# Hybrid decoder trunk on one core: queries left unnormalised until the softmax, and one 512-column product in the channel sub-layers

## The chip, the cores and the metric

One core of one Trainium2 chip runs the whole program in a single launch. The metric is the device time in microseconds (us), the median of several executions; the profile is of one more execution.

## The reference

Two layers work on a sequence of 256 tokens of width 1024, all in float32. Each layer is a mixing sub-layer and a channel sub-layer:

```
h = adaLN(rms_norm(x)); proj = h @ w_in        # q,k,v of A, q,k,v of B, two gates
q_a = rope(rms_norm(q_a), positions)           # rms_norm over each head's 64 numbers
k_a = rope(rms_norm(k_a), positions)           # the same for q_b, k_b
y_a = softmax([mask(q_a k_a^T / 8), sink]) v_a # 8 query heads, 2 key heads, window 128
y_b = softmax(mask(q_b k_b^T / 8)) v_b         # 8 heads, causal (one block of 256)
x  += gt1 * ((sig(gate_a)*(y_a @ w_oA) + sig(gate_b)*(y_b @ w_oB)) @ w_out)
h   = adaLN(rms_norm(x)); x += gt2 * (relu(h @ w_up)**2 @ w_down)   # w_up 1024x4096
```

The scale and the shift of adaLN and the gains gt1, gt2 are products of silu(c) with w_ada (1024x6144 per layer).

## The kernel before, in words

**Precision.** Every large product runs as three products of float32r parts: an operand is split into a high part (a rounded copy) and a low part (the rest). The activations h live transposed in `hT_hi` and `hT_lo`, [128, 8, 256] each; a weight piece of 1024 columns is cast by ScalarE (L440, high part) and subtracted by VectorE (L446, low part) into a slot of 2x1024 numbers. With the activations as moving operand, `mm3f` (L526 to L529) makes high x high, high x low and low x high, each a matmul of 256 columns with its own weight load, all into the same 256 columns of a PSUM tile.

**Feature products.** `feat_half` (L617) makes one block of 128 output features for all 256 tokens: 8 blocks k of the contraction, 3 matmuls each. The gates of the mixing sub-layer are 16 such blocks per layer (L1105); in the channel sub-layer `up` (L1173) makes 2 blocks per step f, for f = 2 to 15, so 28 per layer and 56 in all. `up_done` (L1162) then runs in three stages: Relu from PSUM on ScalarE; Square and a cast to `uhi` on ScalarE; the subtraction to `ulo` on VectorE. `out_product` (L643) makes step f+2 before it multiplies step f by w_down, in 48 matmuls of 512 columns (`out_half`, L522 to L524).

**Queries and keys.** `head_norm_rope` (L735) takes two PSUM tiles (128 tokens each) of a projection: squares on ScalarE (L744), sums by head and an added eps on VectorE (L748, L750), the power -0.5 on GpSimd (L751), the product with it (L758, `qn`), the rotary products (L766 `ra`, L771 `rb`) and their sum (L785 `ro`) on VectorE, and transposes on TensorE (L793). Kinds 0 and 2 are the queries of A and B, 1 and 3 the keys; the gains sit in the rotary tables. `attn_pair` (L799) takes two heads: scores (L810), mask and row maximum (L815, L817), the negated and scaled maximum (L823 or L827), Exp with a constant scale and the maximum as its per-row bias (L830, L832), the row sums, transposes (L854) and the product with v (L870).

**What sets the order.** The bodies are generators on a list `bg`; each `tick()` (L171) inside the large products advances every generator by one stage, splits a weight piece on every second tick, and advances one `ada_unit` (L242) of the list `slow`: VectorE multiplies a w_ada piece of 128x512 by a column of silu(c) and adds it up (L259), 8 steps a unit. A scheduler then orders each engine's queue, so an edit moves rows on every engine. At a boundary between sub-layers `residual` (L637), `ln_stats` (L534) and `ln_apply` (L562) make the next hT from the last products, and `proj_first` (L712) begins the next product with what is ready. All weights come through the one queue of SyncE (`load_next`, L409; `ada_load`, L210).

Of the kernel before, what the change touches and what calls it, by code (L numbers as in the profile page):

```python
# [8 lines left out]
F32 = mybir.dt.float32  # L9
F32R = mybir.dt.float32r  # L10
# [5 lines left out]
P = 128  # L16
S = 256
# [61 lines left out]
def kernel(ctx: ExitStack, tc: tile.TileContext, io):  # L79
# [537 lines left out]
    def feat_half(ahi, alo, ps, k0=0):  # L617

        slot, hi, lo = stream.get()
        for k in range(KT):  # L620
            mm3f(ps, hi[:, k, :], lo[:, k, :], ahi[:, k, :], alo[:, k, :], k == 0, k == KT - 1)
            if k == KT - 1:
                stream.release(slot)
            if k % 4 == 3:
                tick()

    def out_half(accs, half, uhi, ulo, left, k, first, last, ts_, hs_, ticks=True):
        slot, hi, lo = half
# [103 lines left out]
        return ps  # L732


    def head_norm_rope(pss, nh, tabs, kind, dst, p0, dup):  # L735
# [4 lines left out]
        rs = small.tile([P, NT, nh], F32, tag=f"rs{nh}", name=nm("rs"), bufs=2)  # L740
        sqs = []
        for t in range(NT):
            sq = ring(w, "sq")
            nc.scalar.activation(sq, pss[t], AF.Square)  # L744
            sqs.append(sq)
        yield
        for t in range(NT):
            nc.vector.tensor_reduce(out=ss[:, t, :], in_=sqs[t].rearrange("p (h d) -> p h d", d=HD),  # L748
                                    axis=AX.X, op=ALU.add)
        nc.vector.tensor_scalar(out=ss, in0=ss, scalar1=HD * EPS, scalar2=None, op0=ALU.add)  # L750
        nc.gpsimd.tensor_tensor(out=rs, in0=ss, in1=mhalf[:, :NT * nh].rearrange("p (t h) -> p t h", h=nh), op=ALU.pow)  # L751
        for _ in range(POW_LAG):
            yield
        q3s, ab = [], []
        for t in range(NT):
            q3 = ring(w, "qn").rearrange("p (h d) -> p h d", d=HD)
            with tc.issue_after(stream.last):
                nc.vector.tensor_tensor(out=q3, in0=pss[t].rearrange("p (h d) -> p h d", d=HD),  # L758
                                        in1=rs[:, t, :][:, :, None].to_broadcast([P, nh, HD]), op=ALU.mult)
            q3s.append(q3)  # L760
# [36 lines left out]


    def attn_pair(l, pair, qT, kT, v_sb, ahi, alo, alloc):  # L799
# [12 lines left out]
        for i in range(2):  # L812
# [5 lines left out]
                                           in1=(mask[:, 0:2 * P] if swa else mask[:, 2 * P:4 * P]), scale=1.0,  # L818
                                           scalar=NEG, op0=ALU.add, op1=ALU.max, accum_out=mx[:, i, 1:2])
            sms.append(sm)  # L820
        if swa:
            ns = nsink[:, l, 2 * pair:2 * pair + 2][:, :, None].to_broadcast([P, 2, NT])
            nc.vector.scalar_tensor_tensor(out=nmx, in0=mx, scalar=-SCALE, in1=ns, op0=ALU.mult, op1=ALU.min)  # L823
            es = small.tile([P, 2, NT], F32, tag="es", name=nm("es"))
            nc.vector.tensor_tensor(out=es, in0=nmx, in1=ns, op=ALU.subtract)
        else:
            nc.vector.tensor_scalar(out=nmx, in0=mx, scalar1=-SCALE, scalar2=None, op0=ALU.mult)  # L827
        yield
        for i in range(2):
            nc.scalar.activation(sms[i][:, 0:P], sms[i][:, 0:P], AF.Exp, bias=nmx[:, i, 0:1], scale=SCALE,  # L830
                                 accum_out=rsum[:, i, 0:1])
            nc.scalar.activation(sms[i][:, P:3 * P], sms[i][:, P:3 * P], AF.Exp, bias=nmx[:, i, 1:2], scale=SCALE,  # L832
                                 accum_out=rsum[:, i, 1:2])
        if swa:
            nc.scalar.activation(es, es, AF.Exp)
# [205 lines left out]
    def mixing(l, rest, finish):  # L1041
# [118 lines left out]

    def mlp(l, rest, finish, new_u):
        def up_done(uhi, ulo, left, jj, ps):  # L1162
            r = ring(S, "relu")
            nc.scalar.activation(r, ps, AF.Relu)  # L1164
            yield
            u = ring(S, "usq")
            nc.scalar.activation(u, r, AF.Square)
            nc.scalar.copy(uhi[:, jj, :], u)
            yield
            nc.vector.tensor_tensor(out=ulo[:, jj, :], in0=u, in1=uhi[:, jj, :].bitcast(F32), op=ALU.subtract)  # L1170
            left[0] -= 1

        def up(f):  # L1173
            u = new_u()
            for jj in range(2):
                ps = tmp_t()[:, :S]
                feat_half(hT_hi, hT_lo, ps)
                bg.insert(0, up_done(*u, jj, ps))
            return u

# [92 lines left out]
```

## Time and profile before

| | us |
|---|---|
| median of 3 runs | 757.29 |
| the three runs | 754.62, 758.05, 757.29 |
| the profiled execution | 755.65 |
| its span, first to last instruction | 753.9 |

A stretch of the span is named by its start and end, as 226 to 353, in us. In it: the start and the projections of layer 0 (0 to 60), the rest of that mixing sub-layer (60 to 206), its channel sub-layer (206 to 397), the mixing sub-layer of layer 1 (397 to 564) and its channel sub-layer (564 to 754). A matmul's listed duration covers its pipeline, so two neighbours overlap; the step from one start to the next is what it takes of the engine. Rows of waits give the engine that stood idle and what ended it.

### The profile page before, as it was taken

Reading aid. Unit: us, or ns where it says so; the run is one execution under the profiler, and the core shown is the slowest. Engines: PE = TensorE matmul, PEld = TensorE weight load, DVE = VectorE, ACT = ScalarE, POOL = GpSimd, SP = SyncE. Lnnn points to the kernel's source line nnn. Section 1 sums busy time; section 2 is a strip of 40 time slices with the busy share of each in tenths; the row PEclk is TensorE's granted clock in tenths of the full one; section 3 lists DMA queues with packets and bytes.
Section 4 is the critical chain, followed back from the end, with each engine's and each line's share of the span. In section 5 each row is a group of like instructions: output and inputs, shape, how many; then the busy total and the mean of one; then the engine's idle time right before and its main releaser. Section 6 shows DMA issues by size and latency. Waiting matters only on the chain.

```text
span 753.9 us, 12320 instructions
## 1 busy us (share of the span) xinstructions
PE 730.7 (97%) x4713; PEld 645.3 (86%) x4713; DVE 587.2 (78%) x1090; ACT 431.2 (57%) x817; POOL 32.0 (4%) x24
## 2 busy tenths in 40 slices
PE   7999889999999999999999999999999999999997
PEld 6678778899778999989977888989988899999896
DVE  6598998999899988988789788987879745545542
ACT  6545579863466655455436357576447755555550
POOL 1003200000000000000000401000000000000000
PEclk9999999999999999999999999999999999999999
DMA  8996758877949999989882633844662865565501
GB/s 293 392 325 227 227 162 285 274 254 248 303 128 330 370 347 299 332 309 342 283 318 98 224 119 113 263 157 166 225 223 80 269 203 175 182 207 172 189 33 57
DMA packets 110538, 173.46 MB, mean 230 GB/s; under 512 B 4744, under 2 KB 68488, under 8 KB 110480
## 3 DMA queue, kind: packets, MB, share of 16 engines
q1 hardware_dynamic: 109744, 172.54, 67.9%
q8 instruction: 37, 0.61, 0.3%
q10 hardware_dynamic: 736, 0.15, 0.1%
q14 instruction: 21, 0.17, 0.1%
HBM read 171.62 MB, written 1.05 MB: 229 GB/s over the span
## 4 chain that ended last, share of the span: by engine, by line
PE 72%; DVE 13%; DMA 7%; ACT 3%; issue 2%; POOL 2%; SPq 0%; ACTq 0%; DVEq 0%; POOLq 0%
PE tmp L527 11%; PE acc L524 11%; PE acc L522 11%; PE acc L523 11%; PE tmp L528 10%; PE tmp L529 10%; DMA araw<-in_w_ada_dram 4%; DVE ada L259 2%; DVE w L446 2%; PE acc L984 2%; POOL rs L751 1%; ACT w L440 1%; PE tmp L870 1%; DMA wraw<-in_w_up_dram 1%; PE acc L810 1%
## 5 line engine op out<-in xcount | busy, mean ns | idle before, releaser
L446 DVE TENSOR_TENSOR w<-wraw,w 128x1024 fp32r<-128x1024 f32 x137 | 166.3, 1221 | 48.1 <-ACT w L440 46.8
L440 ACT CAST w<-wraw 128x1024 fp32r<-128x1024 f32 x150 | 155.9, 1048 | 78.9 <-PE acc L524 44.5
L527 PE MATMUL tmp<-hT_hi,w 128*128 128x256 f32 x480 | 140.1, 292 | 1.3 <-DVE alo L874 1.2
L529 PE MATMUL tmp<-hT_hi,w 128*128 128x256 f32 x480 | 135.9, 283 | 0.0
L528 PE MATMUL tmp<-hT_lo,w 128*128 128x256 f32 x480 | 135.7, 283 | 0.0
L259 DVE SCALAR_TENSOR_TENSOR ada<-araw,cs,ada 128x512 f32<-128x512 f32 x140 | 104.4, 746 | 3.2 <-DMA araw<-in_w_ada_dram 2.1
L527 PEld LDWEIGHTS tmp<-hT_hi,w 128*128 128x128 f32 x480 | 91.5, 191 | 8.2 <-issue 4.4
L528 PEld LDWEIGHTS tmp<-hT_lo,w 128*128 128x128 f32 x480 | 91.7, 191 | 0.7
L529 PEld LDWEIGHTS tmp<-hT_hi,w 128*128 128x128 f32 x480 | 91.6, 191 | 0.3 <-issue 0.3
L522 PE MATMUL acc<-w,uhi 128*128 128x512 f32 x192 | 75.4, 393 | 0.0
L523 PE MATMUL acc<-w,uhi 128*128 128x512 f32 x192 | 74.9, 390 | 0.0
L524 PE MATMUL acc<-w,ulo 128*128 128x512 f32 x192 | 74.9, 390 | 0.0
L1164 ACT ACTIVATE relu<-tmp 128x256 f32<-128x256 f32 x56 | 21.5, 384 | 68.8 <-PE tmp L529 68.8
L524 PEld LDWEIGHTS acc<-w,ulo 128*128 128x128 f32 x192 | 36.1, 188 | 7.6
L522 PEld LDWEIGHTS acc<-w,uhi 128*128 128x128 f32 x192 | 36.1, 188 | 6.9
L523 PEld LDWEIGHTS acc<-w,uhi 128*128 128x128 f32 x192 | 36.1, 188 | 6.8
L440 ACT CAST kv<-wraw 128x1024 fp32r<-128x1024 f32 x21 | 22.1, 1051 | 24.6 <-PE acc L524 19.8
L446 DVE TENSOR_TENSOR ahi<-wraw,ahi 128x1024 fp32r<-128x1024 f32 x18 | 22.0, 1222 | 15.0 <-ACT ahi L440 14.9
L446 DVE TENSOR_TENSOR kv<-wraw,kv 128x1024 fp32r<-128x1024 f32 x21 | 25.7, 1222 | 9.9 <-ACT kv L440 9.8
L446 DVE TENSOR_TENSOR qT<-wraw,qT 128x1024 fp32r<-128x1024 f32 x21 | 25.6, 1220 | 8.3 <-ACT qT L440 8.3
L527 PE MATMUL tmp<-hT_hi,alo 128*128 128x256 f32 x112 | 31.8, 284 | 0.0
L528 PE MATMUL tmp<-hT_lo,alo 128*128 128x256 f32 x112 | 31.7, 283 | 0.0
(248 smaller groups left out, 1744.8 us busy)
## 6 DMA issues: line engine op xcount, KB each, us to landing
araw<-in_w_ada_dram SPq DMA_DIRECT2D x80, 512.0 KB, 5.9
wraw<-in_w_up_dram SPq DMA_DIRECT2D x32, 1024.0 KB, 5.9
wraw<-in_w_down_dram SPq DMA_DIRECT2D x32, 1024.0 KB, 5.9
wraw<-in_w_in_dram SPq DMA_DIRECT2D x28, 1024.0 KB, 5.7
wraw<-in_w_out_dram SPq DMA_DIRECT2D x8, 1024.0 KB, 5.6
wraw<-in_w_in_dram SPq DMA_DIRECT2D x12, 512.0 KB, 7.1
wraw<-in_w_o_swa_dram SPq DMA_DIRECT2D x8, 512.0 KB, 3.3
wraw<-in_w_o_moba_dram SPq DMA_DIRECT2D x8, 512.0 KB, 5.1
```

Of the source, the lines that this page charges most:

```text
L259: nc.vector.scalar_tensor_tensor(out=acc, in0=raw[:, k, :], scalar=cs[:, kk:kk + 1], in1=(bz if kk == 0 else acc), op0=ALU.mult, op1=ALU.add)
L440: nc.scalar.copy(hi, r)
L446: ins = nc.vector.tensor_tensor(out=lo, in0=r, in1=hi.bitcast(F32), op=ALU.subtract)
L522: nc.tensor.matmul(ps, lhsT=lh, rhs=rh, start=start, stop=False)
L523: nc.tensor.matmul(ps, lhsT=lh, rhs=rl, start=False, stop=False)
L524: nc.tensor.matmul(ps, lhsT=ll, rhs=rh, start=False, stop=stop)
L527: nc.tensor.matmul(ps, lhsT=wh, rhs=ah, start=start, stop=False)
L528: nc.tensor.matmul(ps, lhsT=wh, rhs=al, start=False, stop=False)
L529: nc.tensor.matmul(ps, lhsT=wl, rhs=ah, start=False, stop=stop)
L751: nc.gpsimd.tensor_tensor(out=rs, in0=ss, in1=mhalf[:, :NT * nh].rearrange("p (t h) -> p t h", h=nh), op=ALU.pow)
L984: T.matmul(ps[t], lhsT=left[:, 2 * q + k, t * P:(t + 1) * P], rhs=w[:, k, :], start=(first and k == 0), stop=(last and k == 1))
L1164: nc.scalar.activation(r, ps, AF.Relu)
```

## The change

The activations' parts become one tile, so that both parts of one k lie side by side as 512 columns. `feat_wide` makes high weights times both in one matmul, and low weights times the high part in a second one; `wide_sum` copies the upper half out of PSUM on ScalarE and adds the lower half on VectorE, in two stages. Only `up` uses it: `WIDE_GATE` is False for both layers, so the gates stay as they were. For the queries the product `qn` is left out; the rotary products read PSUM, and the power (now of the sums times 64) goes into the maximum and into Exp as a per-row scale.

```diff
+WIDE_GATE = (False, False)
...
-    hT_hi = state.tile([P, KT, S], F32R, name="hT_hi")
-    hT_lo = state.tile([P, KT, S], F32R, name="hT_lo")
+    hT = state.tile([P, KT, 2, S], F32R, name="hT")
+    hT_hi, hT_lo = hT[:, :, 0, :], hT[:, :, 1, :]
...
+    def feat_wide(ps):
+        slot, hi, lo = stream.get()
+        for k in range(KT):
+            nc.tensor.matmul(ps, lhsT=hi[:, k, :], rhs=hT[:, k].rearrange("p a s -> p (a s)"), start=k == 0, stop=False)
+            nc.tensor.matmul(ps[:, :S], lhsT=lo[:, k, :], rhs=hT_hi[:, k, :], start=False, stop=k == KT - 1)
...
+    def wide_sum(ps, r):
+        nc.scalar.copy(r, ps[:, S:])
+        yield
+        nc.vector.tensor_tensor(out=r, in0=ps[:, :S], in1=r, op=ALU.add)
+        yield
...
+        query = kind % 2 == 0
...
+            if query:
+                nc.vector.tensor_scalar(out=ss, in0=ss, scalar1=HD * EPS, scalar2=1.0 / SCALE ** 2, op0=ALU.add,
+                                        op1=ALU.mult)
+                rq[kind] = rs
...
+        squares()
         q3s, ab = [], []
+        if query:
+            q3s = [p.rearrange("p (h d) -> p h d", d=HD) for p in pss]
+        else:
+            yield
+            powers()
...
         yield
         for t in range(NT):
...
+        if query:
+            powers()
...
+        rp = rq[0 if swa else 2][:, :, h0:h0 + 2].rearrange("p t i -> p i t")
         if swa:
-            nc.vector.scalar_tensor_tensor(out=nmx, in0=mx, scalar=-SCALE, in1=ns, op0=ALU.mult, op1=ALU.min)
+            nc.vector.scalar_tensor_tensor(out=nmx, in0=mx, scalar=-1.0, in1=rp, op0=ALU.mult, op1=ALU.mult)
+            nc.vector.tensor_tensor(out=nmx, in0=nmx, in1=ns, op=ALU.min)
...
-            nc.scalar.activation(sms[i][:, 0:P], sms[i][:, 0:P], AF.Exp, bias=nmx[:, i, 0:1], scale=SCALE,
+            nc.scalar.activation(sms[i][:, 0:P], sms[i][:, 0:P], AF.Exp, bias=nmx[:, i, 0:1], scale=rp[:, i, 0:1],
...
         def up_done(uhi, ulo, left, jj, ps):
-            r = ring(S, "relu")
-            nc.scalar.activation(r, ps, AF.Relu)
-            yield
+            r = ring(S, "usum")
+            yield from wide_sum(ps, r)
+            nc.scalar.activation(r, r, AF.Relu)
...
-                ps = tmp_t()[:, :S]
-                feat_half(hT_hi, hT_lo, ps)
+                ps = tmp_t()
+                feat_wide(ps)
```

**Place 1.** VectorE's queue before, layer 0, from the sums of the squares of `qb` (`ss_623`) and `kb` (`ss_629`) to the rotary products; `acc_282`, `acc_283` hold qb, `acc_284`, `acc_285` kb, `w` is a weight piece's low part.

```order
L748 TENSOR_REDUCE ss_629<-sq_631 128x8
L750 TENSOR_SCALAR ss_623<-ss_623 128x16
L446 TENSOR_TENSOR w_4_647<-wraw_510,w_4_647 128x1024
L748 TENSOR_REDUCE ss_629<-sq_633 128x8
L259 SCALAR_TENSOR_TENSOR ada_721<-araw_722,cs,bz 128x512
L750 TENSOR_SCALAR ss_629<-ss_629 128x16
L446 TENSOR_TENSOR w_4_682<-wraw_510,w_4_682 128x1024
L758 TENSOR_TENSOR qn_687<-acc_282,rs_624 128x512
L758 TENSOR_TENSOR qn_689<-acc_283,rs_624 128x512
L758 TENSOR_TENSOR qn_691<-acc_284,rs_630 128x512
L758 TENSOR_TENSOR qn_693<-acc_285,rs_630 128x512
L766 TENSOR_TENSOR ra_705<-qn_687,ct_463 128x512
```

The same place after the change (qb is `acc_281`, `acc_282`; kb `acc_283`, `acc_284`; the sums of kb are `ss_628`, those of qb `ss_622`):

```order
L805 TENSOR_TENSOR ra_649<-acc_281,ct_462 128x512
L810 TENSOR_TENSOR rb_650<-acc_281,st_463 128x8x32 x2
L447 TENSOR_TENSOR w_4_646<-wraw_509,w_4_646 128x1024
L774 TENSOR_REDUCE ss_628<-sq_630 128x8
L774 TENSOR_REDUCE ss_628<-sq_632 128x8
L805 TENSOR_TENSOR ra_670<-acc_282,ct_462 128x512
L781 TENSOR_SCALAR ss_628<-ss_628 128x16
L810 TENSOR_TENSOR rb_671<-acc_282,st_463 128x8x32 x2
L447 TENSOR_TENSOR w_4_687<-wraw_509,w_4_687 128x1024
L774 TENSOR_REDUCE ss_622<-sq_624 128x8
L774 TENSOR_REDUCE ss_622<-sq_626 128x8
L826 TENSOR_TENSOR ro_696<-ra_649,rb_650 128x512
```

The rotary products of qb stand ahead of the sums, kb's sums ahead of qb's, and the first `ro` of qb ahead of every `qn`.

**Place 2.** ScalarE's queue in the channel sub-layer of layer 0, after the change, for the two blocks of one step (`L641` copies the upper half, `L441` casts a weight piece):

```order
L641 COPY usum_3875<-tmp_3841 128x256
L441 CAST w_19_4028<-wraw_3892 128x1024
L1217 ACTIVATE usum_3875<-usum_3875 128x256
L641 COPY usum_3905<-tmp_3866 128x256
L1219 ACTIVATE usq_3908<-usum_3875 128x256
L441 CAST w_19_4052<-wraw_3892 128x1024
L1220 CAST uhi_3839<-usq_3908 128x256
```

Before, the Relu read PSUM and waited for TensorE alone; now the Relu (L1217) waits for VectorE's sum, and the second block's copy and the next weight cast stand behind it.

**Place 3.** VectorE's queue after the change at the end of that sub-layer, from the normalisation of the first 128 tokens (L553) to that of the second:

```order
L553 TENSOR_SCALAR ln_4097<-x_sb,lnr_4122 128x512 x2
L260 SCALAR_TENSOR_TENSOR ada_4941<-araw_4693,cs,ada_4941 128x512
L581 TENSOR_SCALAR ln_4097<-tmp_4147,s_1_0_99,sh_0_103 128x128 x2
L588 CAST hT<-ln_4097 128x2x128
L659 TENSOR_TENSOR res_4164<-acc_2495,gt_2602 128x512
...
L553 TENSOR_SCALAR ln_4097<-x_sb,lnr_4194 128x512 x2
L260 SCALAR_TENSOR_TENSOR ada_4941<-araw_4693,cs,ada_4941 128x512
L260 SCALAR_TENSOR_TENSOR ada_4941<-araw_4942,cs,ada_4941 128x512
```

Before, no `ada` step stood between these rows: all had been queued ahead of the first L552.

## Rows read from the trace of the kernel before

**Rows 1.** The page's head and part 1: busy time, share of span, instructions.

```profile
span 753.9 us, 12320 instructions
PE 730.7 (97%) x4713; PEld 645.3 (86%) x4713; DVE 587.2 (78%) x1090; ACT 431.2 (57%) x817; POOL 32.0 (4%) x24
```

**Rows 2.** Busy time by stretch: start:end, length, each engine, TensorE's granted clock, DMA share, GB/s.

```profile
60.00:108.00 48.00, 41.75 (x281) 35.55 (x279) 43.28 (x96) 26.16 (x56) 12.48 (x4) 1.00 0.59 191
108.00:165.00 57.00, 55.80 (x465) 50.01 (x461) 51.03 (x135) 48.18 (x132) 0.00 (x0) 1.00 0.81 263
226.00:353.00 127.00, 127.00 (x821) 115.98 (x820) 113.25 (x160) 71.90 (x118) 0.00 (x0) 1.00 0.96 333
353.00:404.00 51.00, 48.37 (x278) 41.84 (x277) 42.73 (x69) 23.72 (x44) 1.47 (x2) 1.00 0.78 271
584.00:735.00 151.00, 151.00 (x969) 137.94 (x968) 78.56 (x91) 86.39 (x142) 0.00 (x0) 1.00 0.55 179
```

**Rows 3.** TensorE in order of time: nine starts at 512 columns, then 47 at 256.

```profile
289.93 0.39 PE L522 MATMUL acc<-kv,uhi 128*128 128x512 f32 x1
...
291.75 0.39 PE L524 MATMUL acc<-kv,ulo 128*128 128x512 f32 x1
...
292.09 0.28 PE L528 MATMUL tmp<-hT_lo,w 128*128 128x256 f32 x1
...
297.61 0.28 PE L529 MATMUL tmp<-hT_hi,w 128*128 128x256 f32 x1
```

**Rows 4.** TensorE's waits, 60 to 108: us in total, times, longest.

```profile
PE tmp L854 <- ACT sm L845: 1.8, 1, 1.8
PE tmp L793 <- DVE ro L785: 1.6, 2, 1.1
PE acc L810 <- DVE qn L758: 1.2, 1, 1.2
PE acc L523 <- DVE w L446: 0.9, 2, 0.6
PE acc L810 <- ACT kv L795: 0.6, 1, 0.6
```

**Rows 5.** VectorE's waits, 60 to 108.

```profile
DVE qn L758 <- POOL rs L751: 4.7, 3, 2.8
```

**Rows 6.** Groups by line and shape: count, busy us, mean ns, idle before.

```profile
L1167 ACT ACTIVATE usq<-relu 128x256 f32<-128x256 f32 x56 | 23.4, 419 | 0.1
L1170 DVE TENSOR_TENSOR ulo<-usq,uhi 128x256 fp32r<-128x256 f32 x56 | 23.4, 418 | 5.1 <-ACT uhi L1168 5.1
L1164 ACT ACTIVATE relu<-tmp 128x256 f32<-128x256 f32 x56 | 21.5, 384 | 68.8 <-PE tmp L529 68.8
L832 ACT ACTIVATE sm<-sm,nmx 128x256 f32<-128x256 f32 x32 | 16.0, 500 | 0.0
L970 ACT ACTIVATE hT_hi<-ln,sh,s 128x256 fp32r<-128x256 f32 x8 | 4.4, 593 | 5.4 <-DVE s L304 5.4
L766 DVE TENSOR_TENSOR ra<-qn,ct 128x512 f32<-128x512 f32 x12 | 8.2, 682 | 0.0
L758 DVE TENSOR_TENSOR qn<-acc,rs 128x512 f32<-128x512 f32 x12 | 7.7, 686 | 11.2 <-POOL rs L751 11.2
L823 DVE SCALAR_TENSOR_TENSOR nmx<-mx,nsink 128x4 f32<-128x4 f32 x8 | 1.3, 158 | 0.1
```

**Rows 7.** VectorE's waits, 226 to 353, the longest, and its group of ulo there.

```profile
DVE w L446 <- ACT w L440: 7.1, 7, 1.9
L1170 DVE TENSOR_TENSOR ulo<-usq,uhi 128x256 fp32r<-128x256 f32 x22 | 9.2, 417 | 0.7 <-ACT uhi L1168 0.7
```

**Rows 8.** The boundary from layer 0 to layer 1, in order of time, with waits.

```profile
397.27 0.66 PE L570 MATMUL tmp<-cpack,ln 128*128 128x128 f32 x4 [2.43 <-DVE ln L552]
404.28 0.73 DVE L580 TENSOR_SCALAR ln<-tmp,s,sh 128x128 f32<-128x128 f32 x2 [0.85 <-PE tmp L570]
```

More of the change, by code (lines that the diff above doesn't have):

```diff
@@ L625, in feat_half @@
                 tick()
+    def feat_wide(ps):
[3 more added lines that the diff above has]
+            nc.tensor.matmul(ps[:, :S], lhsT=lo[:, k, :], rhs=hT_hi[:, k, :], start=False, stop=k == KT - 1)
+            if k == KT - 1:
+                stream.release(slot)
+            if k % 4 == 3:
+                tick()
+    def wide_sum(ps, r):
[3 more added lines that the diff above has]
+        yield
     def out_half(accs, half, uhi, ulo, left, k, first, last, ts_, hs_, ticks=True):
@@ L732, in proj_first @@
         return ps
+    rq = {}
     def head_norm_rope(pss, nh, tabs, kind, dst, p0, dup):
@@ L738, in head_norm_rope @@
         w = nh * HD
+        query = kind % 2 == 0
         ss = small.tile([P, NT, nh], F32, tag=f"ss{nh}", name=nm("ss"), bufs=2)
-        rs = small.tile([P, NT, nh], F32, tag=f"rs{nh}", name=nm("rs"), bufs=2)
+        rs = small.tile([P, NT, nh], F32, tag=("rq" if query else f"rs{nh}"), name=nm("rs"), bufs=2)
         sqs = []
[L742 to L745, printed above, removed]
-        yield
-        for t in range(NT):
-            nc.vector.tensor_reduce(out=ss[:, t, :], in_=sqs[t].rearrange("p (h d) -> p h d", d=HD),
-                                    axis=AX.X, op=ALU.add)
@@ L750, in head_norm_rope, with squares @@
-        nc.vector.tensor_scalar(out=ss, in0=ss, scalar1=HD * EPS, scalar2=None, op0=ALU.add)
-        nc.gpsimd.tensor_tensor(out=rs, in0=ss, in1=mhalf[:, :NT * nh].rearrange("p (t h) -> p t h", h=nh), op=ALU.pow)
-        for _ in range(POW_LAG):
-            yield
[L754 to L760, printed above, removed]
+        def squares():
+            for t in range(NT):
+                sq = ring(w, "sq")
+                nc.scalar.activation(sq, pss[t], AF.Square)
+                sqs.append(sq)
@@ new lines, in powers @@
+        def powers():
+            for t in range(NT):
+                nc.vector.tensor_reduce(out=ss[:, t, :], in_=sqs[t].rearrange("p (h d) -> p h d", d=HD),
+                                        axis=AX.X, op=ALU.add)
+            if query:
[3 more added lines that the diff above has]
+            else:
+                nc.vector.tensor_scalar(out=ss, in0=ss, scalar1=HD * EPS, scalar2=None, op0=ALU.add)
+            nc.gpsimd.tensor_tensor(out=rs, in0=ss, in1=mhalf[:, :NT * nh].rearrange("p (t h) -> p t h", h=nh),
+                                    op=ALU.pow)
@@ new lines, in head_norm_rope @@
+        squares()
+        q3s, ab = [], []
+        if query:
+            q3s = [p.rearrange("p (h d) -> p h d", d=HD) for p in pss]
+        else:
+            yield
+            powers()
+            for _ in range(POW_LAG):
+                yield
+            for t in range(NT):
+                q3 = ring(w, "qn").rearrange("p (h d) -> p h d", d=HD)
+                with tc.issue_after(stream.last):
+                    nc.vector.tensor_tensor(out=q3, in0=pss[t].rearrange("p (h d) -> p h d", d=HD),
+                                            in1=rs[:, t, :][:, :, None].to_broadcast([P, nh, HD]), op=ALU.mult)
+                q3s.append(q3)
@@ L826, in attn_pair @@
         else:
-            nc.vector.tensor_scalar(out=nmx, in0=mx, scalar1=-SCALE, scalar2=None, op0=ALU.mult)
+            nc.vector.scalar_tensor_tensor(out=nmx, in0=mx, scalar=-1.0, in1=rp, op0=ALU.mult, op1=ALU.mult)
         yield
         for i in range(2):
-            nc.scalar.activation(sms[i][:, 0:P], sms[i][:, 0:P], AF.Exp, bias=nmx[:, i, 0:1], scale=SCALE,
+            nc.scalar.activation(sms[i][:, 0:P], sms[i][:, 0:P], AF.Exp, bias=nmx[:, i, 0:1], scale=rp[:, i, 0:1],
                                  accum_out=rsum[:, i, 0:1])
-            nc.scalar.activation(sms[i][:, P:3 * P], sms[i][:, P:3 * P], AF.Exp, bias=nmx[:, i, 1:2], scale=SCALE,
+            nc.scalar.activation(sms[i][:, P:3 * P], sms[i][:, P:3 * P], AF.Exp, bias=nmx[:, i, 1:2], scale=rp[:, i, 1:2],
                                  accum_out=rsum[:, i, 1:2])
@@ L1101, in gate_done @@
         def gate_done(j, ps):
+            if WIDE_GATE[l]:
+                r = ring(S, "gsum")
+                yield from wide_sum(ps, r)
+                ps = r
             nc.scalar.activation(th[:, j, :], ps, AF.Tanh, scale=0.5)
@@ L1105, in mixing @@
         for j in range(16):
-            ps = tmp_t()[:, :S]
-            feat_half(hT_hi, hT_lo, ps)
+            ps = tmp_t()
+            if WIDE_GATE[l]:
+                feat_wide(ps)
+            else:
+                ps = ps[:, :S]
+                feat_half(hT_hi, hT_lo, ps)
             bg.insert(0, gate_done(j, ps))
@@ L1162, in up_done @@
         def up_done(uhi, ulo, left, jj, ps):
-            r = ring(S, "relu")
-            nc.scalar.activation(r, ps, AF.Relu)
-            yield
+            r = ring(S, "usum")
+            yield from wide_sum(ps, r)
+            nc.scalar.activation(r, r, AF.Relu)
             u = ring(S, "usq")
@@ L1175, in up @@
             for jj in range(2):
-                ps = tmp_t()[:, :S]
-                feat_half(hT_hi, hT_lo, ps)
+                ps = tmp_t()
+                feat_wide(ps)
                 bg.insert(0, up_done(*u, jj, ps))
```

1 line of the change is left out of this document (added).

## The prediction, made before the changed kernel had run

> **What bounds the kernel now.** I read the page's head first: TensorE is busy for 730.7 of 753.9 us, VectorE for 587.2, ScalarE for 431.2 [rows 1]. That leaves TensorE at most 23.2 us of visible idleness, so what the kernel does on TensorE sets its time almost everywhere, and a change must either take steps off TensorE or take away one of its few waits. The table by stretches says where these waits lie [rows 2]. From 584 to 735 (the channel sub-layer of layer 1) TensorE never stands still and VectorE is busy for 78.56 of 151 us: whatever leaves TensorE there leaves the time. From 226 to 353 (the same sub-layer of layer 0) TensorE is also full, but VectorE, which does the steps of w_ada there as well, is busy for 113.25 of 127 us and the DMA share is 0.96: there is little room beside TensorE. From 60 to 108 TensorE is busy for 41.75 of 48 us, and this is where the queries and keys of layer 0 are normalised. The granted clock is 1.00 in every stretch, the upper of its two levels, and no row suggests that the change touches it.
>
> Then I looked at what a matmul takes of TensorE. Its listed duration covers its pipeline, so I took the starts [rows 3]: eight steps at 512 columns take 1.82 us, 227.5 ns each; 46 steps at 256 columns take 5.52 us, 120.0 ns each. Two matmuls of 256 columns take 240 ns where one of 512 takes 227.5: 12.5 ns go with the instruction and not with the columns.
>
> **The channel sub-layers: TensorE.** A block had 8 x 3 matmuls of 256 columns; now it has 8 of 512 and 8 of 256. The columns are the same, and 8 instructions are gone, as are their weight loads. There are 56 blocks (28 per layer), so 448 matmuls fewer, each worth 12.5 ns: **5.6 us**, half in each layer. The Trainium skill's "TensorE: Matmul & The Clock Gate", section "Wait — 56ns, not 53.3ns?", speaks against it: a warm matmul costs its columns and a fixed 2.5 ns or so. By that figure the 448 would give an estimated 1.1 us, and the sum below would end at 754.0. This trace disagrees with 12.5 ns, and the sum goes by that.
>
> **The channel sub-layers: what is added.** Per block ScalarE gets one more instruction: the copy from PSUM costs what the Relu from PSUM costs, 384 ns, and the Relu now reads SBUF, as the Square does, at 419 ns [rows 6]. That is 56 x 0.42 = 23.5 us. ScalarE is busy for 71.90 of 127 us from 226 to 353, where 22 blocks would add 9.2 us, and for 86.39 of 151 in layer 1 [rows 2]; TensorE's stream covers it. VectorE gets one addition of 256 columns per block, as the `ulo` subtraction costs: 418 ns [rows 6]. In layer 1 the idle 72 us of VectorE cover it. In layer 0 they are tight: 22 blocks lie between 226 and 353 [rows 7], so 22 x 0.417 = 9.2 us of work go into 127 - 113.25 = 13.75 us of idle time, in a stretch that shrinks by 22 x 8 x 12.5 ns = 2.2 us. That leaves 2.3 us. Most of the idle time is waiting for ScalarE's cast of a weight piece, 7.1 us of it in seven waits of at most 1.9 us [rows 7], and that cast waits for TensorE to free a slot: VectorE is early there, not late, so I take the idle time as usable. But the wait is new (place 2): the Relu stands behind VectorE's sum, and with it the next copy and weight cast; TensorE waits for these last, after it has used up the weight slots already filled.
>
> The scheduler has moved some w_ada steps behind the boundary (place 3). One step of w_ada now stands between the normalised rows and hT for the first 128 tokens, and two for the second. In order they add about 0.67 us (the chain was already late there: TensorE waits 2.43 us for L552 [rows 8]) and 1.3 us less the 0.85 us for which VectorE waited there anyway [rows 8], so 0.5 us. Its saved 2.8 us in layer 0 also reach that boundary as an earlier arrival of TensorE, before a VectorE that has more to do. A bound below is nothing lost; a bound above is that all 2.8 us go and the 1.2 us come on top, 4.0 us. I take **1.5 us lost**, the 1.2 us and a little for the new waits, since the slots hide the rest.
>
> **The queries.** Removed: the product `qn` for the queries, two of 128x512 for each of qa and qb in two layers, 8 x 0.686 = 5.5 us of VectorE [rows 6]. The rotary products then read PSUM; `qn` itself read PSUM and cost 686 ns where `ra` from SBUF cost 682 [rows 6], so they cost the same. Added: one small minimum for each of 8 pairs, 8 x 0.158 = 1.3 us [rows 6]. Moved: the sums and the power, off the chain to the rotary products. In layer 0 VectorE waited 4.7 us for GpSimd's power in three waits [rows 5]; with the four `qn` of that layer, 2.7 us, up to 7.4 us of VectorE's time come back in a stretch where it was busy for 43.28 of 48 us. What TensorE gets of it is bounded by its own waits there [rows 4], 6.1 us in all. The wait for `qn` (1.2) goes, because the rotary products free the projection's PSUM without the power. The waits for `ro` (1.6) go, because qb's `ro` now stands ahead of every `qn` (place 1). Next in line are kb's power, which no longer queues behind qb's on GpSimd, and the weight pieces; of the other 3.3 us I take a third. Bounds: nothing, if kb and the weights take the place of qb at each wait; 6.1 us, if all go. I take **4.0 us**. In layer 1 TensorE is full beside the queries: nothing.
>
> Exp gets a per-row scale beside its per-row bias. The nearest rows are Exp at 256 columns with one per-row operand, 500 ns, and the activation L970 at 256 columns with two, 593 ns [rows 6]: 93 ns for each of 64, 6.0 us of ScalarE. Half fall in layer 0, where ScalarE is busy for 48.18 of 57 us from 108 to 165 [rows 2] but TensorE for 55.80, the gates' products covering it. Bounds: nothing, and the 3.0 us of layer 0 if that cover is gone; I take **0.3 us lost**.
>
> The moved tile adds no copy: hT is written in the same pieces, and I cost it at nothing, since each part still waits for its own writer.
>
> **The sum.** 755.65 - 5.6 + 1.5 - 4.0 + 0.3 = 747.85 us, against the profiled execution (755.65, of which 753.9 is the span). The median of the three runs is 1.64 us above that execution, so I expect a median of **749.5 us**, 1.0% faster. About 0.5%, 3.8 us, is what a measurement of this kernel can tell from no change.
>
> **The rivals.**
>
> *A, the queries give nothing.* VectorE's saved time goes to kb, whose power starts only a little earlier, and to the weight pieces, so TensorE waits as long at other places. For it: two of the five waits are for weight pieces and for kb's transposes copied out (0.9 and 0.6 us [rows 4]). Against it: half of the waits name the queries' own chain. Then 749.5 + 4.0 = 753.5 us, at the edge of no change. Chance 0.19.
>
> *B, the 12.5 ns don't come back.* If the price went with something else than the count of matmuls (the weight's change, which remains twice per k), the 5.6 us shrink to nothing: 755.1 us. Against it: it is the same at 256 and at 512 columns in [rows 3]. Chance 0.05. The Trainium skill's "TensorE: Matmul & The Clock Gate", section named above, would put the kernel near this rival.
>
> *C, VectorE becomes the bound of layer 0's channel sub-layer, and the kernel is slower.* If VectorE's 13.75 us of idle time are forced, because each wait for a cast comes at its place in the queue whatever stands before it, the 9.2 us of sums are added to the stretch, and 6 x 0.42 = 2.5 us to the rest; layer 0 keeps none of its 2.8 us. The sum is 755.65 - 2.8 - 4.0 + 0.3 + 11.7 = 760.85, by the median 762.5 us. It decides from the point where more than 2.3 us of the idle time stay; the whole gain is lost only when some 10 us do. For it: DMA share 0.96 and the new wait of ScalarE on VectorE. Against it: these waits are of an engine that is early. Chance 0.08.
>
> *D, everything goes.* All 6.1 us of the waits, and nothing is lost in layer 0: 755.65 - 5.6 - 6.1 = 743.95, by the median 745.6 us. Chance 0.12.
>
> The forecast has 0.56. The range: from 744.5, a little below D, to 755.5, above A and B; left out are C and what lies between. Faster by over 0.5% (below 753.5): the forecast, D, half of A and a little of the others, 0.78. Slower by over 0.5%: most of C, 0.07. Between: 0.15.
>
> **What would show it.** In the profile after, the starts inside a block should alternate by 227 and 120 ns, and the stretch of layer 1's channel sub-layer should be 2.8 us shorter with TensorE still full. VectorE should show no wait for GpSimd before the rotary products of a query, and TensorE's waits of [rows 4] for `qn` and `ro` should be gone, with under 2.5 us left. Exp should take some 590 ns at 256 columns. In layer 0's channel sub-layer VectorE should be busy for over 95% of the time, and TensorE's wait at the boundary should be 3 to 6 us instead of 2.43. Waits of TensorE for weight pieces inside that sub-layer would mean C; the same total of waits from 60 to 108 would mean A; a step of 240 ns for the wide matmul would mean B.

## The result, and the profile of the changed kernel

The changed kernel takes **752.23 us** (median of 14 runs, 749.42 to 757.62), the kernel before 756.89 (14 runs, 754.62 to 760.76). The ratio is 0.994, with a 95% interval of 0.9916 to 0.9964: 4.7 us, or 0.6%. The forecast was 749.5 with a range of 744.5 to 755.5. The direction and the range hold; of the 7.8 us that the sum had gained, some 3 are missing. The profiled execution took 750.69 us.

The page's head and part 1, which answer to [rows 1]:

```profile
span 748.9 us, 11477 instructions
PE 732.1 (98%) x4265; PEld 625.1 (83%) x4265; DVE 603.6 (81%) x1146; ACT 451.6 (60%) x873; POOL 33.3 (4%) x24
```

TensorE has 448 matmuls fewer (4713 to 4265), and only 16.8 us of visible idleness instead of 23.2. VectorE and ScalarE work 16.4 and 20.4 us more. The stretches, columns as in [rows 2]:

```profile
60.00:108.00 48.00, 46.01 (x320) 40.16 (x319) 48.00 (x111) 31.39 (x69) 10.10 (x4) 1.00 0.70 231
108.00:165.00 57.00, 55.48 (x453) 49.53 (x452) 48.28 (x129) 47.97 (x123) 0.00 (x0) 1.00 0.74 250
226.00:353.00 127.00, 127.00 (x652) 107.76 (x651) 120.14 (x180) 78.78 (x139) 0.00 (x0) 1.00 0.94 327
...
584.00:735.00 151.00, 151.00 (x759) 127.67 (x758) 87.00 (x110) 90.43 (x164) 0.00 (x0) 1.00 0.53 172
```

From 60 to 108 TensorE is busy for 46.01 us where it was 41.75, and all of its waits there are these, against the five of [rows 4]:

```profile
PE acc L851 <- ACT kv L836: 0.8, 1, 0.8
PE acc L851 <- DVE mx L858: 0.8, 1, 0.8
PE tmp L898 <- ACT sm L889: 0.3, 1, 0.3
```

The waits for `qn` and `ro` are gone, 6.1 us have become 1.9, and VectorE waits for GpSimd nowhere in that stretch [rows 5]. In layer 0's channel sub-layer VectorE is busy for 120.14 of 127 us and TensorE never stands still. The added instructions, groups by line as in [rows 6]:

```profile
L1217 ACT ACTIVATE usum<-usum 128x256 f32<-128x256 f32 x56 | 23.3, 417 | 7.5 <-DVE usum L643 7.5
...
L641 ACT COPY usum<-tmp 128x256 f32<-128x256 f32 x56 | 20.8, 372 | 67.0 <-PE tmp L634 67.0
L876 ACT ACTIVATE sm<-sm,nmx,rs 128x256 f32<-128x256 f32 x32 | 18.9, 592 | 0.0
```

```profile
L643 DVE TENSOR_TENSOR usum<-tmp,usum 128x256 f32<-128x256 f32 x56 | 23.6, 422 | 26.5 <-ACT usum L641 26.3
```

Copy 372, sum 422, Relu 417, Exp 592 ns: each within 13 ns of the row it was priced by. The last columns are new waits between the two engines (VectorE 26.3 us for the copy, ScalarE 7.5 for the sum); TensorE, which has its slots filled ahead, waits for neither. At the two boundaries, TensorE in order of time:

```profile
205.42 1.09 PE L571 MATMUL tmp<-cpack,ln 128*128 128x128 f32 x8 [2.37 <-DVE ln L553]
...
392.66 0.63 PE L571 MATMUL tmp<-cpack,ln 128*128 128x128 f32 x4 [0.49 <-DVE ln L553]
```

The second answers to [rows 8]: 0.49 us instead of 2.43, where 3 to 6 had been forecast. The first, within layer 0, I had not looked at; it was 1.70 us in the kernel before (at 207.53), and 2.43 in a second profile of it. And in layer 1, sixteen pairs of a wide and a narrow product (two blocks):

```profile
599.73 0.39 PE L633 MATMUL tmp<-hT,w 128*128 128x512 f32 x1
599.96 0.28 PE L634 MATMUL tmp<-hT,w 128*128 128x256 f32 x1
...
605.37 0.40 PE L523 MATMUL acc<-w,uhi 128*128 128x512 f32 x1
```

(605.37 - 599.73) / 16 = 352.5 ns a pair. By [rows 3] it was to be 227.5 + 120.0 = 347.5, and three narrow products were 360.

### The profile page after: what moved, and what is told of

It reads as the page before. It is cut to its first block, busy times and chain, and to the rows that moved or that the text cites. A ratio compares the mean times of both kernels' runs of the same rounds, so it can differ in the third digit from the quotient of the medians.

```text
span 748.9 us, 11477 instructions
## 1 busy us (share of the span) xinstructions
PE 732.1 (98%) x4265; PEld 625.1 (83%) x4265; DVE 603.6 (81%) x1146; ACT 451.6 (60%) x873; POOL 33.3 (4%) x24
## 4 chain that ended last, share of the span: by engine, by line
PE 83%; DVE 11%; DMA 3%; issue 2%; ACT 1%; POOL 0%; ACTq 0%; DVEq 0%; POOLq 0%; SPq 0%
PE tmp L633 14%; PE acc L523 12%; PE acc L525 12%; PE acc L524 12%; PE tmp L634 7%; PE tmp L528 5%; PE tmp L529 4%; PE tmp L530 4%; PE acc L1028 3%; DVE w L447 2%; DVE ada L260 2%; PE tmp L914 2%; DMA araw<-in_w_ada_dram 1%; PE acc L851 1%; PE tmp L898 1%
## 5 line engine op out<-in xcount | busy, mean ns | idle before, releaser
L441 ACT CAST w<-wraw 128x1024 fp32r<-128x1024 f32 x150 | 155.8, 1048 | 78.4 <-PE acc L525 41.5
L633 PE MATMUL tmp<-hT,w 128*128 128x512 f32 x224 | 80.1, 399 | 0.0
L528 PE MATMUL tmp<-hT,w 128*128 128x256 f32 x256 | 76.7, 299 | 1.5 <-DVE alo L918 1.5
L530 PE MATMUL tmp<-hT,w 128*128 128x256 f32 x256 | 72.4, 283 | 0.1
L529 PE MATMUL tmp<-hT,w 128*128 128x256 f32 x256 | 72.3, 282 | 0.0
L634 PE MATMUL tmp<-hT,w 128*128 128x256 f32 x224 | 62.9, 281 | 0.0
L641 ACT COPY usum<-tmp 128x256 f32<-128x256 f32 x56 | 20.8, 372 | 67.0 <-PE tmp L634 67.0
L528 PEld LDWEIGHTS tmp<-hT,w 128*128 128x128 f32 x256 | 48.6, 190 | 8.3 <-issue 5.3
L633 PEld LDWEIGHTS tmp<-hT,w 128*128 128x128 f32 x224 | 42.1, 188 | 10.0
L530 PEld LDWEIGHTS tmp<-hT,w 128*128 128x128 f32 x256 | 48.7, 190 | 0.7 <-DVE w L447 0.7
L529 PEld LDWEIGHTS tmp<-hT,w 128*128 128x128 f32 x256 | 48.7, 190 | 0.4 <-issue 0.2
L643 DVE TENSOR_TENSOR usum<-tmp,usum 128x256 f32<-128x256 f32 x56 | 23.6, 422 | 26.5 <-ACT usum L641 26.3
L634 PEld LDWEIGHTS tmp<-hT,w 128*128 128x128 f32 x224 | 42.3, 189 | 0.5
L633 PE MATMUL tmp<-hT,alo 128*128 128x512 f32 x112 | 40.3, 399 | 0.0
```

The source lines that it names most:

```text
L441: nc.scalar.copy(hi, r)
L528: nc.tensor.matmul(ps, lhsT=wh, rhs=ah, start=start, stop=False)
L529: nc.tensor.matmul(ps, lhsT=wh, rhs=al, start=False, stop=False)
L530: nc.tensor.matmul(ps, lhsT=wl, rhs=ah, start=False, stop=stop)
L633: nc.tensor.matmul(ps, lhsT=hi[:, k, :], rhs=hT[:, k].rearrange("p a s -> p (a s)"), start=k == 0, stop=False)
L634: nc.tensor.matmul(ps[:, :S], lhsT=lo[:, k, :], rhs=hT_hi[:, k, :], start=False, stop=k == KT - 1)
```

## The experiments

Ratios are to the kernel before on the same chip. The rows come from three chips' runs, four rows each, with 6 or 12 runs a row; the medians of the kernel before there were 758.1, 756.31 and 757.34 us.

| kernel | median us | ratio | 95% interval |
|---|---|---|---|
| the kernel before, again | 758.58 | 1.0001 | 0.9979 to 1.0023 |
| queries' part alone | 754.84 | 0.9972 | 0.9949 to 0.9995 |
| wide products alone | 755.80 | 0.9971 | 0.9949 to 0.9994 |
| change, eight wide then eight narrow | 752.05 | 0.9928 | 0.9902 to 0.9954 |
| change, Exp with a constant scale | 746.95 | 0.9854 | 0.9811 to 0.9896 |
| eight and eight, w_ada held at each boundary | 747.80 | 0.9871 | 0.9824 to 0.9917 |
| eight and eight, gates of layer 1 wide | 749.05 | 0.9869 | 0.9818 to 0.9919 |
| eight and eight, w_ada held, gates wide | 748.76 | 0.9887 | 0.9839 to 0.9934 |
| the change, again | 750.46 | 0.9911 | 0.9879 to 0.9942 |
| change, Exp with a per-row constant | 752.50 | 0.9938 | 0.9914 to 0.9962 |
| eight and eight, w_ada held in layer 0 only | 747.52 | 0.9879 | 0.9850 to 0.9909 |
| the same, gates of layer 1 wide | 747.90 | 0.9880 | 0.9849 to 0.9912 |

**The kernel before, again**, with no edit.

> The kernel before, unchanged, to see its own clock run by run. Theory: the lower granted clock that the profile of the change shows (0.992 over the span, 0.78 to 0.85 between 10 and 30 us and 0.83 from 205 to 215) is not the change's doing: the kernel before has runs below 1.000 as often, its profile with 1.000 was one of several. Rival: the change brings it, through TensorE's longer idle time ahead of the channel sub-layer of layer 0 (2.37 us instead of 1.70); then every run here shows 0.998 to 1.000. Ratio 1.000 either way, within 0.3%.

TensorE's granted clock (the number ahead of the last two) from 10 to 20 and from 205 to 226 us, in the kernel before run again:

```profile
10.00:20.00 10.00, 6.61 (x46) 5.86 (x44) 8.28 (x15) 7.91 (x13) 0.97 (x1) 0.87 1.06 379
205.00:226.00 21.00, 18.00 (x82) 14.09 (x81) 19.57 (x42) 12.60 (x27) 1.61 (x2) 0.92 0.42 125
```

and in the change:

```profile
10.00:20.00 10.00, 7.25 (x44) 6.64 (x43) 7.35 (x14) 7.07 (x12) 0.98 (x1) 0.81 1.05 372
205.00:226.00 21.00, 19.84 (x97) 16.41 (x98) 19.59 (x43) 14.03 (x29) 0.61 (x1) 0.92 0.40 132
```

The theory holds. The kernel before falls to the lower level in the same two places; the profile that the rows before the prediction come from, with 1.00 in both, was one of its better executions in that respect. The change does not bring the lower clock, and the clock is not most of the missing 3 us: at equal clock, by the line of the last section, the change gains 5.5 us instead of 4.7.

The change itself, run again, was expected at a ratio of 0.994, between 0.9915 and 0.9965. It came out at 0.9911, a little below that range; its interval (0.9879 to 0.9942) and that of the first 14 runs (0.9916 to 0.9964) overlap.

**Each part alone.** The first has `up` and its end as before:

```
-                feat_wide(ps)
+                feat_half(hT_hi, hT_lo, ps)
...
```

> The queries' part alone; the channel sub-layers keep three products of 256 columns. Theory (the two parts add, as the trace of the change reads): layer 0's attention 3.4 us shorter, 1.0 us given back where VectorE is late at the boundary to the channel sub-layer, layer 1's attention 1.0 us longer because of the slower Exp: net -1.4 us, ratio 0.998. Rival 1 (the prediction's price): -3.7 us, ratio 0.995, with layer 1 unchanged. Rival 2: the 1.0 us lost in layer 1 come from the channel sub-layers' new order ahead of it; then layer 1's attention is not longer here.

The second has `head_norm_rope` and `attn_pair` of the kernel before.

> The wide products alone; the queries are normalised as before. Theory: -1.6 us in each channel sub-layer by the steps of TensorE, and about -1.9 us of TensorE's wait at the boundary to layer 1, because VectorE's steps of w_ada stand behind its row work there: -5.1 us, ratio 0.993. Rival 1 (the prediction): -2.8 in layer 1, -1.3 in layer 0, the wait at the boundary grown to 3 to 6 us: -4.1 us, ratio 0.9946. Rival 2: the boundary's gain hangs on the queries' part (an earlier arrival): then the wait there stays at 2.4 us and the sum is -3.2 us, ratio 0.996.

The ratios, 0.9972 and 0.9971, make -2.1 and -2.2 us: both parts help, and about equally, where the prediction had -3.7 and -4.1. The first comes out between its theory and rival 1, and its interval holds both; its rival 2 falls, for layer 1's attention is no shorter with the narrow products (77.71 us, 77.70 in the change). The second gains less than its theory and both rivals said, though its interval holds rival 2's 0.996. Both traces show the boundary to layer 1, first the queries' part, then the wide products:

```profile
396.37 0.66 PE L571 MATMUL tmp<-cpack,ln 128*128 128x128 f32 x4 [0.40 <-DVE ln L553]
```

```profile
398.02 0.63 PE L571 MATMUL tmp<-cpack,ln 128*128 128x128 f32 x4 [0.49 <-DVE ln L553]
...
438.44 0.39 PE L524 MATMUL tmp<-w,hT 128*128 128x256 f32 x1 [1.59 <-DVE w L447]
```

So either part alone removes the wait, and rival 2 of the wide products falls as to the wait. What had made it, by the traces, stands on VectorE. First the profile of [rows 8], then the kernel before run again, where the wait was 2.07 us:

```profile
386.98 1.54 DVE L259 SCALAR_TENSOR_TENSOR ada<-araw,cs,ada 128x512 f32<-128x512 f32 x2 [1.62 <-DMA araw<-in_w_ada_dram]
...
389.58 0.68 DVE L640 TENSOR_TENSOR res<-acc,gt 128x512 f32<-128x512 f32 x1
```

```profile
393.91 1.54 DVE L259 SCALAR_TENSOR_TENSOR ada<-araw,cs,ada 128x512 f32<-128x512 f32 x2 [1.59 <-DMA araw<-in_w_ada_dram]
395.36 0.68 DVE L640 TENSOR_TENSOR res<-acc,gt 128x512 f32<-128x512 f32 x1
```

A step of w_ada waits for its transfer (1.62 and 1.59 us) with residuals of the boundary behind it. In the change, and with either part alone, no step waits for a transfer there, and VectorE is early enough to wait for TensorE (0.77 us in the change, for the residual at 390.17). No run changes that order alone, so this cause is read from the traces. The wide products alone give the gain back in layer 1: there VectorE still waits for the power of normalised queries, and TensorE 1.59 us (438.44) for a weight piece behind it. From that boundary to the transposes of `relu` in layer 1 they take 189.70 us, where the kernel before took 185.16 and 186.46 in its two profiles and the change 186.42. In the whole change the wait of 1.59 us does not occur.

**Eight wide products first, then eight narrow ones.**

```
         for k in range(KT):
             nc.tensor.matmul(ps, lhsT=hi[:, k, :], rhs=hT[:, k]..., start=k == 0, stop=False)
+            if k == 5:
+                tick()
+        for k in range(KT):
             nc.tensor.matmul(ps[:, :S], lhsT=lo[:, k, :], rhs=hT_hi[:, k, :], ...)
-            if k == KT - 1:
-                stream.release(slot)
-            if k % 4 == 3:
-                tick()
+        stream.release(slot)
+        tick()
```

> The whole change, but a block does its eight products of 512 columns first and then its eight of 256 (same products, same sums). In the change a pair of one and one takes 353 ns, not 227.5 + 120 = 347.5. Theory: it is the turn from one width to the other that costs 5.5 ns a pair; here the steps are 227.5 and 120.0 ns inside the runs of eight, a block takes 2.78 us instead of 2.82, and 56 blocks give 2.3 us, ratio to before 0.991. Rival: the wide product itself costs more than a product of 512 columns elsewhere (its data, its two halves): steps of 232 to 237 ns stay, a block takes 2.82 us, and the time is that of the change, 0.994.

Layer 1's channel sub-layer runs from its transposes of `relu` to the last matmul. The queries' part alone, which has the three narrow products there:

```profile
582.76 1.04 PE L1244 MATMUL tmp<-cpack,relu 128*128 128x128 f32 x8
...
749.50 0.39 PE L525 MATMUL acc<-w,ulo 128*128 128x512 f32 x1
```

The change:

```profile
579.08 1.03 PE L1244 MATMUL tmp<-cpack,relu 128*128 128x128 f32 x8
...
744.20 0.39 PE L525 MATMUL acc<-w,ulo 128*128 128x512 f32 x1
```

Eight and eight, with two blocks in a row:

```profile
576.83 1.04 PE L1245 MATMUL tmp<-cpack,relu 128*128 128x128 f32 x8
...
675.23 1.98 PE L633 MATMUL tmp<-hT,ahi 128*128 128x512 f32 x8
677.04 1.11 PE L637 MATMUL tmp<-hT,ahi 128*128 128x256 f32 x8
677.99 2.00 PE L633 MATMUL tmp<-hT,alo 128*128 128x512 f32 x8
679.83 1.11 PE L637 MATMUL tmp<-hT,alo 128*128 128x256 f32 x8
680.78 0.40 PE L523 MATMUL acc<-qT,uhi 128*128 128x512 f32 x1
...
741.01 0.39 PE L525 MATMUL acc<-w,ulo 128*128 128x512 f32 x1
```

166.74, 165.12 and 164.18 us. TensorE is full in all three, so this is the products' price and nothing else: 224 matmuls fewer give 1.62 us when wide and narrow alternate (7.2 ns each) and 2.56 us when they don't (11.4 ns). In runs of eight the steps are 226 to 230 ns at 512 columns and 119 at 256, and two blocks take 5.55 us, 347 ns a pair: what [rows 3] had promised. In the change two blocks took 5.64 (599.73 to 605.37). So the theory holds and the rival falls: it is the turn from width to width that takes back a third of the 12.5 ns. Why a turn costs anything stays open. Whole-kernel ratios of 0.9928 and 0.994 cannot tell the two apart; the stretches can. The Trainium skill's "TensorE: Matmul & The Clock Gate", section "Wait — 56ns, not 53.3ns?", with about 2.5 ns a matmul, would give an estimated 0.56 us for these 224; neither order agrees.

**The price of Exp.** With a constant scale, and with a per-row column that holds the constant, both with the old maximum step:

```
-            nc.scalar.activation(..., AF.Exp, bias=nmx[:, i, 0:1], scale=rp[:, i, 0:1], ...
+            nc.scalar.activation(..., AF.Exp, bias=nmx[:, i, 0:1], scale=SCALE, ...
```

> The change, with the softmax as before: Exp with one constant scale and the old maximum step. This leaves out the queries' norms, so its output is not the attention's. It prices the slower Exp (593 instead of 500 ns, 64 times) and the eight small minima. Theory: layer 0 hides them, layer 1's attention is 1.0 us shorter than in the change (77.7 us from its first score product to the first product of the mixing; the kernel before 76.7), ratio to the change 0.9987. Rival 1 (the prediction): 0.3 us, not to be measured, and the 77.7 us stay. Rival 2: the Exp of layer 0 is on TensorE's path too: 3 us, ratio to before 0.990.

```
+            nc.scalar.activation(..., AF.Exp, bias=nmx[:, i, 0:1], scale=cscale, ...
```

> The change with the old maximum step, and with Exp's scale read per row, but from a column that holds the constant. This leaves out the queries' norms, so its output is not the attention's. It splits what the change with one constant scale gained over the change (some 4 us): the 64 slower Exp are in it here, the eight small minima and the wait for the queries' power are not. Theory: the per-row scale is the price, Exp takes 593 ns at 256 columns, and the time is that of the change to within 1 us, ratio to before 0.993. Rival: the wait for the queries' power and the minima are the price; then the time is that with the constant scale, 4 us under the change, ratio 0.988, although Exp takes 593 ns.

ScalarE's Exp at 256 columns, constant, then per-row:

```profile
L875 ACT ACTIVATE sm<-sm,nmx 128x256 f32<-128x256 f32 x32 | 15.9, 496 | 0.0
```

```profile
L877 ACT ACTIVATE sm<-sm,nmx,cscale 128x256 f32<-128x256 f32 x32 | 18.9, 592 | 0.0
```

The two ratios, 0.9854 and 0.9938, have intervals that don't meet, and the second lies with the change (0.994, 0.9911). (The interval of the change run again, from 0.9879, does meet that of the constant, up to 0.9896.) So the theory of the second run holds: the per-row scale is the price, not the minima nor the wait for the power. Of the first run's expectation the theory (1.0 us, layer 1 alone) falls and rival 2 comes nearest: layer 0 pays too. With the constant, TensorE reaches the boundary inside layer 0 at 201.72 instead of 205.42, though its first product of the projections starts 0.28 us later (19.20, not 18.92):

```profile
201.72 0.66 PE L571 MATMUL tmp<-cpack,ln 128*128 128x128 f32 x4 [1.33 <-DVE ln L553]
```

and from 108 to 165 it is all but full, where the change had 55.48 us:

```profile
108.00:165.00 57.00, 56.93 (x474) 51.61 (x473) 50.57 (x131) 47.21 (x123) 0.00 (x0) 1.00 0.80 268
```

What the change waits for there is `alo`, the low part of the attention's output, TensorE's only wait of the stretch (us in total, times, longest):

```profile
PE tmp L528 <- DVE alo L918: 1.5, 1, 1.5
```

VectorE at that place, in order of time, in the change:

```profile
113.98 0.75 DVE L260 SCALAR_TENSOR_TENSOR ada<-araw,cs,ada 128x512 f32<-128x512 f32 x1 [1.66 <-DMA araw<-in_w_ada_dram]
114.65 1.22 DVE L447 TENSOR_TENSOR w<-wraw,w 128x1024 fp32r<-128x1024 f32 x1
115.79 0.42 DVE L918 TENSOR_TENSOR alo<-tmp,ahi 128x256 fp32r<-128x256 f32 x1
```

with the constant scale:

```profile
113.01 0.41 DVE L917 TENSOR_TENSOR alo<-tmp,ahi 128x256 fp32r<-128x256 f32 x1
114.18 0.75 DVE L260 SCALAR_TENSOR_TENSOR ada<-araw,cs,ada 128x512 f32<-128x512 f32 x1 [0.76 <-DMA araw<-in_w_ada_dram]
```

and with the per-row constant:

```profile
117.26 0.75 DVE L260 SCALAR_TENSOR_TENSOR ada<-araw,cs,ada 128x512 f32<-128x512 f32 x1 [3.60 <-DMA araw<-in_w_ada_dram]
...
119.06 0.42 DVE L919 TENSOR_TENSOR alo<-tmp,ahi 128x256 fp32r<-128x256 f32 x1
```

With the slower Exp the scheduler puts `alo` behind a step of w_ada that waits for its transfer; with the quick one, ahead of it. The transfer lands at about 114 us in the change and with the constant, so a kernel whose VectorE is early, as the change's is, waits longer there: TensorE waited 1.5 us in the change, 2.5 in its second profile and 3.5 with the per-row constant. After the two longer waits TensorE's clock was lower too: from 118 to 130 it was 1.00 in the change, 0.97 in its second profile, and with the per-row constant 0.72:

```profile
118.00:130.00 12.00, 10.46 (x56) 8.82 (x57) 8.80 (x24) 5.03 (x17) 0.00 (x0) 0.72 0.48 146
```

Two things limit this reading. The kernel before, with the quick Exp, also had TensorE wait once for `alo` in that stretch:

```profile
PE tmp L527 <- DVE alo L874: 1.2, 1, 1.2
```

There it stood behind VectorE's own work, and the wait was 0.7 us in its second profile. So part of what the constant takes away the kernel before had too, at a later place. And the 3.7 us (205.42 less 201.72) are one pair of profiles: 1.5 of them are this wait and 1.0 is the shorter wait at the boundary (1.33 instead of 2.37), which was 1.11 in the change's second profile. How much of the price is the order, and how much ScalarE's own 3 us in layer 0, was not separated. Layer 1's attention (first score product to first product of the mixing) is 77.70 us in the change, 77.66 in its second profile, and 76.50 with the constant; the kernel before had 76.70 and 77.99 in its two profiles, so that 1.2 us is not certain.

**Versions.** The steps of w_ada in a channel sub-layer held behind the boundary's last write of hT, and the gates of layer 1 as wide products (`WIDE_GATE = (False, True)`), both on top of eight and eight:

```
+                with tc.issue_after(stream.behind[1]) if stream.behind else ExitStack():
...
                     nc.vector.scalar_tensor_tensor(out=acc, in0=raw[:, k, :], ...
```

> Eight wide products first, then eight narrow ones, and the steps of w_ada that belong to a channel sub-layer are held until the boundary's last write of hT on VectorE. In the change two of them (0.74 us each) stand among the row work at the boundary from the mixing to the channel sub-layer of layer 0, where TensorE waits for VectorE's ln for 1.7 to 2.4 us. Theory: this wait is where part of the queries' gain is given back; without the two steps it falls by 1.3 to 1.5 us to under 1 us, and VectorE catches up in the channel sub-layer; ratio to before 0.991 where the same kernel without the hold gave 0.9928. Rival: VectorE has no room in layer 0's channel sub-layer (120 of 127 us busy), the steps come late at its end, the wait at the boundary to layer 1 grows by the same 1.5 us, and nothing is gained.

> Eight wide products first, and the gates' products of layer 1 made the same way: 16 blocks more. Theory: TensorE gains 16 x 0.09 = 1.5 us, and VectorE, busy for 53.5 of 60 us there, takes the 16 sums (6.7 us) in the later part, where the gates go on after the attention: ratio to before 0.991. Rival: the sums stand ahead of the maxima and the norms of the softmax on VectorE, TensorE waits for the attention's work instead, and the time is that without it, 0.993, or 2 us more, 0.9955.

> Both of the last two together: the steps of w_ada held at the boundary, and wide products for the gates of layer 1. Theory: the two gains add, 3 us below the kernel with eight wide products first alone, ratio to before 0.989. Rival: one of them gives nothing, 0.991; both give nothing, 0.993.

The hold shortens layer 0's channel sub-layer (166.96 us from its transposes to the boundary to layer 1; 168.15 without), so the rival there falls. But it holds layer 1's steps as well, and TensorE then waits in layer 1:

```profile
PE tmp L276 <- ACT ghi L272: 1.0, 1, 1.0
PE tmp L277 <- DVE glo L273: 0.2, 1, 0.2
```

Its sub-layer there takes 166.13 us instead of 164.18. The wide gates shorten layer 1's attention from 77.70 to 76.92 us, half of what was expected; the ratio, 0.9869, says more than that, but its interval is 0.010 wide. Together they don't add: that attention takes 79.93 us, and 78.75 with the hold alone. So the hold was limited to layer 0 (`if u in ADA_PLAN[1]`):

> Eight wide products first, then eight narrow ones, with the steps of w_ada held behind the boundary from the mixing to the channel sub-layer of layer 0 only; held in layer 1 too, the gates' products there waited for late casts and lost 3 us. Theory: TensorE's wait for ln at that boundary falls under 1.5 us, the channel sub-layer of layer 0 is not longer than 168 us, layer 1 stays as with eight wide products first alone (164.2 us for its channel sub-layer): ratio 0.9905, 1.5 to 2 us under that kernel. Rival: the held steps come back at the boundary to layer 1, as a wait of 2 us or more, ratio 0.993.

> The same with wide products for layer 1's gates as well, all that helped so far. Theory: 0.8 to 1.5 us more than the last, ratio 0.989; layer 1's attention 77 us. Rival: the held steps and the gates' sums meet on VectorE in layer 1, the attention there is 78 us or more, and the ratio is 0.9905 or above.

With it layer 0's sub-layer keeps its gain,

```profile
224.82 0.71 PE L1246 MATMUL tmp<-cpack,relu 128*128 128x128 f32 x5
...
391.82 0.38 PE L572 MATMUL tmp<-cpack,ln 128*128 128x128 f32 x2
```

167.00 us, and layer 1's is 164.20. The wait inside layer 0 did not fall under 1.5 us in the first (2.2; 1.4 in the second), and layer 1's attention with wide gates took 76.90 us. Medians of 747.52 and 747.90 us, ratios 0.9879 and 0.9880, lie with the lowest of those that compute the whole, and their stretches say why; beside the change on the same chip (750.46, 0.9911) their intervals still overlap, so the times alone don't show that they are faster than the change. The wide gates add nothing to the time here, where 0.8 to 1.5 us more had been expected.

## Why the prediction was right or wrong

**The bound.** Right: TensorE sets the time, and what left it in a full stretch left the time. It was not the whole of it: two of the three misses below come, at least in part, from waits that the order of VectorE's queue made or removed.

**The matmuls, -5.6 us.** The mechanism was right, the size not: 1.62 us in layer 1, and 1.46 in layer 0, where the sub-layer took 170.46 us with the queries' part alone and 169.00 in the change with the same short wait at its end. That is -3.1. The step that failed is "each worth 12.5 ns": the two steps of [rows 3] were each measured in a run of one width, and the change alternates them, at 7.2 ns. With the widths kept apart the same step holds nearly whole (11.4 ns in layer 1). Rival B, that nothing comes back, is wrong too.

**What is added, +1.5 us.** The durations were right and the cover held: VectorE at 94.6% in layer 0's sub-layer (over 95% was forecast), no wait of TensorE inside it; rival C did not occur. The boundary was wrong in sign: 2.43 us of waiting became 0.49, about -1.9. This step failed: I had counted the steps of w_ada that the change puts behind the boundary, and not asked what they had held up ahead of it.

**The queries, -4.0 us.** Right: TensorE's waits from 60 to 108 fell by 4.2 us (by 3.4 against the second profile of the kernel before, which had 5.3), 2.8 of it by the two chains named; so neither rival A nor D occurred. That layer 1 gets nothing from it holds against the kernel before; the wide products alone, with the queries still normalised, met a new wait of 1.59 us there.

**Exp, +0.3 us.** This step failed most. The 93 ns were right (592 against 500; the Trainium skill's "ScalarE: Activation LUTs", section "What ACT_TABLE_LOAD costs", has about 93 ns for a per-row operand, and the trace agrees), but "the gates' products covering it" was not: by the trace 3.7 us up to the boundary inside layer 0, and perhaps 1.2 in layer 1. The upper bound, 3.0 us, counted ScalarE's time alone; the order that follows from it, with `alo` behind a transfer on VectorE, lies outside it. The trace before had shown the place, TensorE's 1.2 us for `alo`, and I did not read it.

**The sum**: -3.1 - 1.9 - 4.2 + 3.7 to 4.9 = -5.5 to -4.3 us, with 4.7 measured; the parts are read from single profiles. The first three, -9.2, can be held against the change with the constant scale, which leaves Exp out: its profile is 9.8 us shorter than that of the kernel before, and its ratio makes 11.0 us (7.9 to 14.3). Two errors of one sign (2.5 and 3.4 to 4.6) and one of the other (3.4) left the total inside the range. That is luck in good part: its parts were further off than the total.

## What to carry to other kernels

A price taken from a run of equal instructions holds for such a run: when a change mixes shapes, measure the mixture, or keep equal shapes together. An engine with idle time is no cover by that alone; ask which instruction stands behind the slower one in each queue, and whether a step that waits for a transfer now stands ahead of it. Where steps move across a boundary, count what they leave as well as what they join.

## What the runs showed of the hardware that I had not expected

On TensorE a 512-column and a 256-column product in turn took 352.5 ns, against 347 in runs of eight (347.5 by the steps of [rows 3]); over the whole sub-layer of layer 1 the difference between the two orders was 0.94 us.

The granted clock differs from one execution to the next of one kernel: 0.985 to 0.998 over the span in most runs of the kernel before, 0.984 to 1.000 in the change's. A straight line through the runs of all kernels (those at 0.98 and above) gives some 0.55 us per 0.001, and at equal clock the change is 5.5 us (plus or minus 0.9) faster. From 205 to 226 us it was 0.84 in the profile of the wide products alone, after a wait of 3.0 us, 0.92 in the change and in the kernel before run again, after 2.4 us, and 1.00 in the queries' part alone, after 1.4; but also 1.00 with w_ada held in layer 0, after 2.2 us, and after some 1.7 us it was 1.00 in the kernel before and 0.92 with eight and eight. So the length of the wait alone does not say it.
